# A hybrid attention and mLSTM layer on one core: remainders move from GpSimd to VectorE, row tiles by token halves, and the merge's seven products in another order

## The chip, the cores and the metric

One core of a Trainium2 chip runs the whole kernel. The metric is the device time of one execution in microseconds (us), as the median of several runs. Beside it stands the span of one profiled execution, from its first instruction to its last. The engines are named as in the profile: PE multiplies matrices, PEld loads its weights, DVE (VectorE) and ACT (ScalarE) work element by element, POOL is GpSimd, SP only issues DMAs.

## The reference

One layer on 1024 tokens of width 1024, all in float32:

```python
h = rms_norm(x) * (1 + sc_a) + sh_a                 # scales and shifts from the conditioning c
aq, ak, av, mq, mk, mv, mo, mi, mf, ga, gm = split(h @ w_in)
ya = diff_attention(...)                            # 8 heads, two softmaxes each, causal, with a bias
hm = mlstm_chunkwise(...)                           # 4 heads, matrix memory, after a short convolution of mq, mk
ym = sigmoid(mo) * rms_norm(hm)
merged = sigmoid(ga) * (ya @ w_a) + sigmoid(gm) * (ym @ w_m)
x = x + gt_a * (merged @ w_out)
h = rms_norm(x) * (1 + sc_f) + sh_f
x = x + gt_f * (square(relu(h @ w_ff1)) @ w_ff2)    # 1024 -> 4096 -> 1024
```

## The kernel before, in words

**Three products for one.** PE multiplies in a rounded format (fp32r). To keep float32's accuracy every operand is split in two: ACT writes the rounded high part, and a subtraction `src - high` makes the remainder (`split_lo`, L138). A product then costs three matmuls: high by high, high by remainder, remainder by high (`mm3` L165 to L167, `mm_block` L327). The subtraction runs on DVE or on POOL. `split_lo` takes an argument: true means POOL, false DVE, and none means every second one on POOL. Its callers `parts`, `add` and `sub` pass none through `pick`, which keeps two running loads and gives POOL a piece whenever DVE's load is well ahead.

**Weights of the projections.** `load_w` (L147 to L153) loads two stages `w_st` of 128x1024 by DMA, lets ACT write `w_hi` and subtracts into `w_lo`. `plan` is a list of such loads, and each product that takes its weights starts the next load. The entries of `plan` for the branch gates, for the queries and keys of each attention head (`qk_cols`), for the last values and for `w_m` say POOL.

**Seven products for eight.** The large products use Winograd's form of Strassen's scheme: a product of 2x2 blocks of 512 is made by seven block products, numbered 1 to 7, with sums of operand blocks before and sums of results behind them. The class `Group` does it for the projections and the first feed-forward product, the class `Chunks` for the merge product `ya @ w_a`, for `merged @ w_out` and for the second feed-forward product. A `Chunks` has a list of jobs, one per block product. `prep` makes the operand sums of a job and splits both operands into one of two sets of buffers (`s_op`, `t_op`); `run` lets PE do its 48 matmuls of 128x512 and calls `out` for each of four PSUM banks. The loop preps job n+1 before it runs job n, so a job's splits wait for the job two before it to release the buffers. Products 1, 5, 6 and 7 start new banks, 2, 3 and 4 accumulate on those of 1, 5 and 7.

**Orders.** The merge and the second feed-forward product run `ORDER_X` = (1, 7, 2, 4, 5, 6, 3), the product with `w_out` runs `ORDER_Y` = (1, 2, 5, 6, 3, 7, 4). `operands` has both sets of sums. In the merge, `out_a` adds the products into four quadrants of `merged` and calls `merge` for each piece: it fetches the gate and the other branch's part by DMA, takes a tanh on ACT, and does one multiply (L1288) and one add on DVE. For `w_out`, `out_o` adds into the rows `xr` of x, squares on ACT, and `rms` scales the rows for the next norm. `pieces` loads quadrants of weights, and multiplies those of `w_out` by the gate `gta` on DVE (L1672).

**Stages in time.** The norm of x and its transposed rows `hT`; projections as `Group`s until about 510 us; the four mLSTM heads until about 750 us; the eight attention heads until about 1290 us, each with the projection of the next head's queries and keys between its steps (`weave`); during the last head and after it the product of `ym` with `w_m`; the merge, the product with `w_out`, the first and the second feed-forward product.

**Row tiles.** `ActX` holds `hT` and later `ym` as four tiles of one pool with four buffers. A tile holds one part (high or remainder), four of the eight row blocks of 128 features, and all 1024 tokens. `reload` (L1273 to L1277) reads `ym` back from memory, a pair of row blocks and one token half at a time, as soon as `hT`'s buffers are free.

**Between the norm and the feed-forward products.** `norm_feat` transposes the scaled rows, `half0` splits them into the operands of products 1 and 2, and `right` makes the operand sums of the products 7, 5, 6, 3 and 4 (L312, then `parts`). These sums and splits go through `pick`. The order of this part is written out by hand as a string of letters.

The program is unrolled; a scheduler puts each engine's instructions in an order and adds the semaphores. An engine takes its own instructions in order.

Of the kernel before, what the change touches and what calls it, by code (L numbers as in the profile page):

```python
# [36 lines left out]
def kernel(  # L37
# [131 lines left out]
    class ActX:  # L169


        def __init__(self, name):
            self.t = [[xp.tile([P, 4, S], F32R, name=f"{name}{r}{i}", tag="x") for i in range(2)] for r in range(2)]

        def at(self, k, t0, n):
            return tuple(self.t[r][k // 4][:, k % 4, t0:t0 + n] for r in range(2))
# [350 lines left out]
    def modulate(q):  # L527
# [15 lines left out]
        def step(n):  # L543
# [9 lines left out]
            hh, hl = (hT.t[r][q][:, k:k + 2, m * 256:(m + 1) * 256] for r in range(2))  # L553
# [205 lines left out]
    class Conv(Group):  # L759
# [9 lines left out]
        def out(self, t, hf, n, a, b, into):  # L769
            c = crow[t][:, hf * 512:hf * 512 + 512]  # L770
            if b is None:
                nc.scalar.activation(c, a, AF.Copy)
            else:
                add(c, a, b, None if (t, hf) == (1, 1) else False)
            if (t, hf) in ((0, 1), (1, 0)):
                behind.extend(self.conv(t))
# [25 lines left out]
    class Gate(Group):  # L802
# [9 lines left out]
        def out(self, t, hf, n, a, b, into):  # L812
# [3 lines left out]
            if b is None:  # L816
                nc.scalar.activation(c, a, AF.Copy)
            else:
                add(c, a, b, None if (t, hf) == (1, 1) else False)
# [39 lines left out]
    def ml_in(h, hd):  # L859


        def half(hf):
# [7 lines left out]
            for i in (1, 0):  # L870
                for t in range(2):
                    d = hd["qk"][i, t, hf] = wt("r", [P, 2, 512], "qk", F32R)
                    parts((d[:, 0, :], d[:, 1, :]), hd["kc"][t][:, ts_] if i else q[:, t, :])

        def vals(g):
# [7 lines left out]
            parts((vt[:, :, 0, 0:256], vt[:, :, 1, 0:256]), vr)  # L883
# [212 lines left out]
    def at_v(h, vts):  # L1096
# [3 lines left out]
        def read(g):  # L1100
# [3 lines left out]
            parts((vt[:, :, 0, :], vt[:, :, 1, :]), vr.rearrange("p t (a d) -> p (t a) d", a=2))  # L1104
# [212 lines left out]
    def gate_cols(i):  # L1317
        cols((C_GA, C_GM)[i // 4] + (i % 4) * 256, True)

    def qk_cols(h):  # L1320
# [3 lines left out]
        plan.append(lambda: load_w([(srcs[q], lambda v, q=q: v[:, :, q * P:(q + 1) * P]) for q in range(2)], KT, True))  # L1324
# [6 lines left out]
    for h in range(AH):  # L1331
        if h % 2 == 0 and h // 2 not in (0, 1, 2):
            cols(C_AV + h * P, True)
# [4 lines left out]
    for u in range(4):  # L1338
        plan.append(lambda u=u: load_cols(w_m[0], u * 256, True))
# [142 lines left out]
    for h in range(AH):  # L1482
# [18 lines left out]
    class Chunks:  # L1501
# [6 lines left out]
        def __init__(self, xs):  # L1508
            self.n, self.jobs, self.made, self.tmp = 0, [], 0, {}
# [15 lines left out]
        def add(self, order, left, right, out, sums=None):  # L1525
            self.jobs += [(i, order, left, right, out, sums) for i in order]
# [9 lines left out]
        def prep(self):  # L1536
# [5 lines left out]
            i, order, left, right, _, sums = self.jobs[n]  # L1542
            s, t = self.s[n % 2], self.t[n % 2]
            for q in range(2):
                l, r = self.operands(i, order[1] == 7, left, right, sums, q)
                self.split(s(q), l)
                self.split(t(q), r)

        def operands(self, i, x, left, right, sums, q):
            b11, b12, b21, b22 = (right.get((m, q)) for m in (11, 12, 21, 22))  # L1550
            if sums is None:
                a11, a12, a21, a22 = (left[m, q] for m in (11, 12, 21, 22))
            two = range(2)

            def tmp(tag, name):
                return [wt(tag, [P, 512], name) for _ in two]
# [4 lines left out]
            r = {1: b11, 2: b21, 3: b22, 4: b21, 5: b12, 6: b11, 7: b12}[i]  # L1561
            if x:
                if i == 7:
                    r = tmp("f", "t3")
                    for k in two:
# [5 lines left out]
            elif i == 5:  # L1571
                r = self.tmp["r", q] = tmp("f", "t1")
                for k in two:
                    sub(r[k], b12[:, k], b11[:, k], False)
            elif i == 6:
                minus(b12, b22, b12)
                for k, v in enumerate(self.tmp["r", q]):
                    sub(b11[:, k], b22[:, k], v, False)
            elif i == 4:
                minus(b21, b21, b11)  # L1580
            if sums is not None:
                return sums(i, q), r
            l = {1: a11, 2: a12, 3: a12, 4: a22, 5: a21, 6: a11, 7: a21}[i]
            if i == 3:
                minus(a12, a12, a11)
            elif x:
                if i == 7:
                    l = tmp("m", "s3")
                    for k in two:
                        sub(l[k], a11[:, k], a21[:, k], False)  # L1590
                elif i == 5:
                    add(a21, a21, a22, False, 2)
                elif i == 6:
                    minus(a11, a21, a11)
            elif i == 5:
                l = self.tmp["l", q] = tmp("m", "s1")
                for k in two:
                    add(l[k], a21[:, k], a22[:, k], False)
            elif i == 6:
                minus(a21, a11, a21)  # L1600
                for k, v in enumerate(self.tmp["l", q]):
                    sub(a11[:, k], v, a11[:, k], False)
            return l, r

        def run(self):

            i, order, _, _, out, _ = self.jobs[self.n]
# [21 lines left out]
    ORDER_Y = (1, 2, 5, 6, 3, 7, 4)  # L1629
# [52 lines left out]
    def out_a(i, j, ps):  # L1682
        f0, f1 = j * P, 512 + j * P
        if i == 1:
            nc.scalar.activation(u1[:, j], ps, AF.Copy)
        elif i == 7:
            nc.scalar.activation(m22[:, j], ps, AF.Copy)
        elif i == 2:
            merge(m11[:, j], ps, f0, 0)
        elif i == 4:  # L1690
            add(m12[:, j], ps, u1[:, j], False)
        elif i == 5:
            add(m22[:, j], ps, m22[:, j], False)
            add(m22[:, j], m22[:, j], u1[:, j], False)
        elif i == 6:
# [384 lines left out]
```

## Time and profile before

| | |
|---|---|
| median of 3 runs | 2135.2 us (2126.42 to 2137.53) |
| the profiled execution | 2137.04 us, of which the span is 2135.2 us |
| mean granted TensorE clock | 0.970 |
| HBM read, written | 206.43 MB, 79.93 MB |
| queue q1 (hardware DMAs) | 41.8% of the DMA engines' time |

The page of the profile gives each engine's busy time, then the span in 40 slices, then the chain of work that ended last. Answers of the trace give the same by window of time, by group of equal instructions (how many, busy us, mean ns of one, idle time before them and what ended it) and one by one in order of time. A busy PE is not PE at its peak: back-to-back matmuls overlap in the records.

### The profile page before, as it was taken

What the parts mean: (1) busy time and instruction counts of PE and PEld (TensorE: products, weight loads), DVE (VectorE), ACT (ScalarE), POOL (GpSimd) and SP (SyncE); (2) the same over time, 40 slices, a digit from 0 to 9 for tenths busy, and PEclk for the clock granted to TensorE, in tenths of its full rate; (3) what the DMA queues carried; (4) which work ended last, traced back from release to release, by engine and by line L of the source; (5) the groups of instructions that cost most, each with busy time, mean ns of one, the idle gap of its engine ahead of it and who ended that gap; (6) DMA issues with size and microseconds to landing.
All of it is one profiled execution on the core that took longest, in us unless ns stands there. A gap on an engine that the chain in (4) does not pass through costs nothing. (4 is left out here: it accounts for less than half of the span.)

```text
span 2135.2 us, 30324 instructions
## 1 busy us (share of the span) xinstructions
PE 2001.3 (94%) x11201; PEld 1732.3 (81%) x11201; DVE 1660.5 (78%) x2887; ACT 1045.5 (49%) x1966; POOL 234.0 (11%) x251
## 2 busy tenths in 40 slices
PE   5889999999889999999999999888799999899999
PEld 5889898888778899898988788677678888788887
DVE  7876668987765468989877747998777667898896
ACT  5522234444565557777756634435444555433332
POOL 0000000002232211111112410004400000000000
PEclk7999999999999999999999999999899999999999
DMA  8354453235655342222222665503344445845432
GB/s 284 111 163 156 150 162 118 91 107 193 192 177 162 107 122 60 80 60 80 60 66 69 202 222 169 171 1 123 114 169 156 153 148 201 305 139 167 150 117 80
DMA packets 210634, 296.72 MB, mean 139 GB/s; under 512 B 14067, under 2 KB 132494, under 8 KB 210486
## 3 DMA queue, kind: packets, MB, share of 16 engines
q1 hardware_dynamic: 207542, 285.35, 41.8%
q0 software_dynamic: 2944, 9.44, 1.2%
q8 instruction: 88, 1.44, 0.3%
q14 instruction: 60, 0.49, 0.1%
HBM read 206.43 MB, written 79.93 MB: 134 GB/s over the span
## 5 line engine op out<-in xcount | busy, mean ns | idle before, releaser
L327 PE MATMUL cps<-t_op,s_op 128*128 128x512 f32 x2016 | 478.4, 398 | 27.3 <-ACT s_op L319 10.9
L327 PEld LDWEIGHTS cps<-t_op,s_op 128*128 128x128 f32 x2016 | 383.1, 191 | 119.6 <-ACT s_op L319 12.6
L319 ACT ACTIVATE w_op<-w_st 128x512 fp32r<-128x512 f32 (+1 forms) x192 | 130.6, 695 | 183.8 <-PE pb L327 57.8
L138 DVE TENSOR_TENSOR w_op<-w_st,w_op 128x512 fp32r<-128x512 f32 (+1 forms) x192 | 146.7, 784 | 6.3 <-ACT w_op L319 4.1
L165 PE MATMUL ps<-w_hi,hT 128*128 128x256 f32 x512 | 146.9, 287 | 0.0
L166 PE MATMUL ps<-w_lo,hT 128*128 128x256 f32 x512 | 146.7, 286 | 0.0
L167 PE MATMUL ps<-w_hi,hT 128*128 128x256 f32 x512 | 146.2, 286 | 0.0
L319 ACT ACTIVATE s_op<-act 128x1024 fp32r<-128x1024 f32 x56 | 58.4, 1051 | 142.9 <-PE cps L327 108.0
L138 POOL TENSOR_TENSOR w_lo<-w_st,w_hi 128x1024 fp32r<-128x1024 f32 x36 | 87.9, 2453 | 313.3 <-ACT w_hi L152 310.0
L1198 ACT ACTIVATE ee<-ee,mneg 128x256 f32<-128x256 f32 (+7 forms) x128 | 98.4, 770 | 21.0 <-DVE mneg L1194 20.6
L327 PE MATMUL pa<-b,w_op 128*128 128x512 f32 x384 | 96.4, 402 | 6.7 <-ACT m L430 6.6
L1188 PE MATMUL lg<-kb,qe 128*128 128x512 f32 (+3 forms) x384 | 96.1, 361 | 4.2 <-DVE kb L1160 1.9
L327 PE MATMUL pc<-bt,w_op 128*128 128x512 f32 x384 | 96.1, 396 | 3.8 <-DVE w_op L138 2.0
L166 PEld LDWEIGHTS ps<-w_lo,hT 128*128 128x128 f32 x512 | 98.0, 191 | 1.5 <-issue 0.9
L165 PEld LDWEIGHTS ps<-w_hi,hT 128*128 128x128 f32 x512 | 97.9, 191 | 0.8
L167 PEld LDWEIGHTS ps<-w_hi,hT 128*128 128x128 f32 x512 | 98.0, 191 | 0.2
L327 PEld LDWEIGHTS pa<-b,w_op 128*128 128x128 f32 x384 | 74.1, 194 | 23.1 <-ACT m L430 7.6
L327 PEld LDWEIGHTS pc<-bt,w_op 128*128 128x128 f32 x384 | 71.1, 188 | 24.6 <-DVE w_op L138 7.0
L315 DVE TENSOR_TENSOR acc<-cps,acc 128x512 f32<-128x512 f32 x116 | 76.9, 684 | 13.0 <-PE cps L327 12.8
L715 DVE SCALAR_TENSOR_TENSOR ac<-crow,cond,ac 128x256 f32<-128x256 f32 x112 | 54.0, 482 | 34.2 <-DMA crow<-in_w_ada_dram 32.5
L1194 DVE CUSTOM_DVE_ANT_0 ee<-lg,bs 128x512 f32<-128x512 f32 (+4 forms) x128 | 70.1, 559 | 12.4 <-PE lg L1188 11.4
L138 DVE TENSOR_TENSOR s_op<-act,s_op 128x1024 fp32r<-128x1024 f32 x56 | 68.2, 1219 | 5.4 <-ACT s_op L319 5.3
(418 smaller groups left out, 4948.8 us busy)
## 6 DMA issues: line engine op xcount, KB each, us to landing
w_st<-in_w_in_dram SPq DMA_DIRECT2D x72, 512.0 KB, 4.5
act<-act_d SPq DMA_DIRECT2D x56, 512.0 KB, 3.6
w_st<-in_w_ff_dram SPq DMA_DIRECT2D x36, 512.0 KB, 4.1
crow<-in_w_ada_dram SPq DMA_DIRECT2D x32, 512.0 KB, 3.9
w<-in_w_ff_dram SPq DMA_DIRECT2D x32, 512.0 KB, 5.0
act_d<-s SPq DMA_DIRECT2D x48, 256.0 KB, 2.0
wa<-in_w_ada_dram SPq DMA_DIRECT2D x16, 512.0 KB, 4.8
mq_d<-cv SPq DMA_DIRECT2D x16, 512.0 KB, 2.8
```

The source lines that it names most:

```text
L138: return (nc.gpsimd if pool else nc.vector).tensor_tensor(dst, src, hi.bitcast(F32), op=ALU.subtract)
L165: nc.tensor.matmul(o, lhsT=ah, rhs=bh, start=first, stop=False)
L166: nc.tensor.matmul(o, lhsT=ah, rhs=bl, start=False, stop=False)
L167: nc.tensor.matmul(o, lhsT=al, rhs=bh, start=False, stop=last)
L315: (nc.gpsimd if pick(pool, n) else nc.vector).tensor_tensor(o, a, b, op=ALU.add)
L319: nc.scalar.activation(dst[0], src, AF.Copy)
L327: nc.tensor.matmul(ps, lhsT=p, rhs=q, start=first and k == 0 and r == 0, stop=k == 3 and r == 2, skip_group_check=True,)
L715: nc.vector.scalar_tensor_tensor(ac, stv[:, k, :], cond[:, kk:kk + 1], ac, op0=ALU.mult, op1=ALU.add)
L1188: nc.tensor.matmul(lg[:, 0:max(256, w)], lhsT=hd["q"][hf][e][:, r, q4 * P:(q4 + 1) * P], rhs=hd["k"][e][:, c0:c0 + max(256, w)], start=r = ...
L1194: nc.vector.tensor_tensor_reduce(ee[:, c0:c0 + w], lg[:, 0:w], hd["bs"][:, n - c0 - w:n - c0][:, ::-1], -0.125, first, ALU.add, ALU.min, last,
L1198: nc.scalar.activation(ee[:, 0:n], ee[:, 0:n], AF.Exp, bias=mneg[:, e:e + 1], scale=-1.0, accum_out=ssum[:, e:e + 1])
```

## The change

- `split_lo`, `parts`, `add` and `sub` are told to use DVE wherever they were told to use POOL or were free to choose: the weights in `plan`, the reload of `ym`, the operands of the mLSTM heads, the values of attention, `half0` and `right`.
- `ActX` has one tile for each token half and part, with all eight row blocks.
- The merge runs (1, 2, 6, 7, 4, 5, 3), the product with `w_out` runs (1, 2, 6, 5, 3, 7, 4); the second feed-forward product stays as it was. All the sums of product 6 are made at its prep, in place but for one pair `t2`: those that its own operands need first, and three more (`behind`) after its splits. Product 7 then needs one more sum.
- In the merge the results are added 5 times for each column block instead of 7, and the four calls of `merge` come one at each of the products 2, 4, 5 and 3. For `w_out` it is 9 additions instead of 11, and one copy on ACT.
- The quadrants of `w_out` are loaded in the order 11, then 21, 12, 22.

```diff
 class ActX:
-            self.t = [[xp.tile([P, 4, S], F32R, name=f"{name}{r}{i}", tag="x") for i in range(2)] for r in range(2)]
+            self.t = [[xp.tile([P, KT, 512], F32R, name=f"{name}{r}{i}", tag="x") for r in range(2)] for i in range(2)]
...
-                    parts((d[:, 0, :], d[:, 1, :]), hd["kc"][t][:, ts_] if i else q[:, t, :])
+                    parts((d[:, 0, :], d[:, 1, :]), hd["kc"][t][:, ts_] if i else q[:, t, :], False)
...
-        cols((C_GA, C_GM)[i // 4] + (i % 4) * 256, True)
+        cols((C_GA, C_GM)[i // 4] + (i % 4) * 256, False)
...
-        plan.append(lambda u=u: load_cols(w_m[0], u * 256, True))
+        plan.append(lambda u=u: load_cols(w_m[0], u * 256, False))
...
-            filler += reload(ym, ym_d, True) + units[0:12 * 2]
+            filler += reload(ym, ym_d, False) + units[0:12 * 2]
...
+            a11, a12, a21, a22 = (left[m, q] for m in (11, 12, 21, 22))
+            l = {1: a11, 2: a12, 3: a12, 4: a22, 5: a21, 6: a11, 7: a11}[i]
+            r = {1: b11, 2: b21, 3: b22, 4: b21, 5: b12, 7: b11}.get(i)
+            if i == 6:
+                add(a21, a21, a22, False, 2)
+                minus(a11, a21, a11)
+                minus(b12, b12, b11)
+                r = [wt("f", [P, 512], "t2") for _ in range(2)]
+                for k in range(2):
+                    sub(r[k], b22[:, k], b12[:, k], False)
+                def rest():
+                    for k in range(2):
+                        sub(b21[:, k], b21[:, k], r[k], False)
+                        sub(b11[:, k], r[k], b11[:, k], False)
+                    minus(a12, a12, a11)
+                behind = (rest,)
+            elif i == 7:
+                minus(a11, a22, a11)
...
-    ORDER_Y = (1, 2, 5, 6, 3, 7, 4)
+    ORDER_Y = (1, 2, 6, 7, 4, 5, 3)
+    ORDER_Z = (1, 2, 6, 5, 3, 7, 4)
...
 def out_a(i, j, ps):
         elif i == 4:
             add(m12[:, j], ps, u1[:, j], False)
+            merge(m12[:, j], m12[:, j], f1, 0)
         elif i == 5:
             add(m22[:, j], ps, m22[:, j], False)
             add(m22[:, j], m22[:, j], u1[:, j], False)
-        elif i == 6:
-            add(m12[:, j], ps, m12[:, j], False)
-            add(m22[:, j], ps, m22[:, j], False)
-            add(u1[:, j], ps, u1[:, j], False)
-            merge(m12[:, j], m12[:, j], f1, 0)
             merge(m22[:, j], m22[:, j], f1, 512)
+        elif i == 6:
+            add(u1[:, j], ps, u1[:, j], False)
...
 def out_o(i, j, ps):
+                elif i == 6:
+                    add(u2[:, j], ps, u2[:, j], False)
                 elif i == 5:
-                    add(hi[:, c1], ps, hi[:, c1], False)
-                    for q in (lo[:, c1], hi[:, c0], hi[:, c1]):
-                        add(q, q, u2[:, j], False)
-                elif i == 6:
-                    for q in (lo[:, c1], hi[:, c0], hi[:, c1]):
-                        add(q, ps, q, False)
+                    nc.scalar.activation(u1[:, j], ps, AF.Copy)
                 elif i == 3:
+                    add(lo[:, c1], lo[:, c1], u2[:, j], False)
                     add(lo[:, c1], ps, lo[:, c1], False)
...
                 elif i == 7:
-                    add(hi[:, c1], ps, hi[:, c1], False)
+                    add(hi[:, c1], hi[:, c1], u2[:, j], False)
+                    add(u1[:, j], ps, u1[:, j], False)
+                    add(hi[:, c1], hi[:, c1], u1[:, j], False)
                     square(4 + j, 1)
                 else:
+                    add(hi[:, c0], hi[:, c0], u2[:, j], False)
                     add(hi[:, c0], ps, hi[:, c0], False)
...
 def half0(k):
-        parts(B[1 + k // 4](k % 4), e_at(k))
+        parts(B[1 + k // 4](k % 4), e_at(k), False)
...
-            sub(b21, b21, b22)
-        parts(B[i](k), src)
+            sub(b21, b21, b22, False)
+        parts(B[i](k), src, False)
```

More of the change, by code (lines that the diff above doesn't have):

```diff
@@ L552, in step @@
                     pin(nc.scalar.activation(vi, vi, AF.Identity, bias=b, scale=g))
-            hh, hl = (hT.t[r][q][:, k:k + 2, m * 256:(m + 1) * 256] for r in range(2))
+            ks = slice(q * 4 + k, q * 4 + k + 2)
+            hh, hl = (hT.t[m // 2][r][:, ks, m % 2 * 256:m % 2 * 256 + 256] for r in range(2))
             pin(nc.scalar.activation(hh, v, AF.Copy))
@@ L1323, in qk_cols @@
         ]
-        plan.append(lambda: load_w([(srcs[q], lambda v, q=q: v[:, :, q * P:(q + 1) * P]) for q in range(2)], KT, True))
+        plan.append(lambda: load_w([(srcs[q], lambda v, q=q: v[:, :, q * P:(q + 1) * P]) for q in range(2)], KT, False))
     AT_GATES = {}
@@ L1525, in add @@
         def add(self, order, left, right, out, sums=None):
-            self.jobs += [(i, order, left, right, out, sums) for i in order]
+            self.jobs += [(i, left, right, out, sums) for i in order]
         def split(self, dst, src):
@@ L1541, in prep, with operands @@
             self.made += 1
-            i, order, left, right, _, sums = self.jobs[n]
+            i, left, right, _, sums = self.jobs[n]
             s, t = self.s[n % 2], self.t[n % 2]
             for q in range(2):
-                l, r = self.operands(i, order[1] == 7, left, right, sums, q)
+                l, r, behind = self.operands(i, left, right, sums, q)
                 self.split(s(q), l)
                 self.split(t(q), r)
-        def operands(self, i, x, left, right, sums, q):
+                run(behind)
+        def operands(self, i, left, right, sums, q):
             b11, b12, b21, b22 = (right.get((m, q)) for m in (11, 12, 21, 22))
[L1551 to L1556, printed above, removed]
             def minus(o, a, b):
                 sub(o, a, b, False, 2)
-            r = {1: b11, 2: b21, 3: b22, 4: b21, 5: b12, 6: b11, 7: b12}[i]
-            if x:
+            if sums is not None:
+                r = {1: b11, 2: b21, 3: b22, 4: b21, 5: b12, 6: b11, 7: b12}[i]
                 if i == 7:
-                    r = tmp("f", "t3")
-                    for k in two:
+                    r = [wt("f", [P, 512], "t3") for _ in range(2)]
+                    for k in range(2):
                         sub(r[k], b22[:, k], b12[:, k], False)
@@ L1603, in operands @@
-            return l, r
+                return sums(i, q), r, ()
+            a11, a12, a21, a22 = (left[m, q] for m in (11, 12, 21, 22))
+            l = {1: a11, 2: a12, 3: a12, 4: a22, 5: a21, 6: a11, 7: a11}[i]
+            r = {1: b11, 2: b21, 3: b22, 4: b21, 5: b12, 7: b11}.get(i)
+            behind = ()
+            if i == 6:
[6 more added lines that the diff above has]
+                def rest():
+                    for k in range(2):
+                        sub(b21[:, k], b21[:, k], r[k], False)
[4 more added lines that the diff above has]
+                minus(a11, a22, a11)
@@ L1605, in run @@
+            return l, r, behind
         def run(self):
-            i, order, _, _, out, _ = self.jobs[self.n]
+            i, _, _, out, _ = self.jobs[self.n]
             s, t = self.s[self.n % 2], self.t[self.n % 2]
@@ L1711 @@
         if n == 4:
-            wo = pieces("e", "wo", w_out[0], False, (11, 12), behind)
+            wo = pieces("e", "wo", w_out[0], False, (11,), behind)
         ch.run()
         if n == 5:
-            pieces("v", "wo", w_out[0], False, (21, 22), behind, wo)
+            pieces("v", "wo", w_out[0], False, (21,), behind, wo)
+            pieces("e", "wo", w_out[0], False, (12,), behind, wo)
+            pieces("v", "wo", w_out[0], False, (22,), behind, wo)
             xr = fetch("r", "xr", x2, range(8))
```

60 lines of the change are left out of this document (14 added, 46 removed).

## The prediction

> **What bounds the kernel now.** I read the page first: the busy shares, then the slices of PE, DVE and POOL.
>
> ```profile
> PE 2001.3 (94%) x11201; PEld 1732.3 (81%) x11201; DVE 1660.5 (78%) x2887; ACT 1045.5 (49%) x1966; POOL 234.0 (11%) x251
> PE   5889999999889999999999999888799999899999
> DVE  7876668987765468989877747998777667898896
> POOL 0000000002232211111112410004400000000000
> ```
>
> PE bounds most of the span, and where its slice reads 9 nothing on DVE or POOL can move the time. It falls off at the start, in the mLSTM heads, in the last attention head, and in four slices from 1335 us on. DVE stands at 9 before those, POOL at 4 within. Next, the windows of these stages.
>
> ```profile
> 800.00:1100.00 300.00, 286.70 (x2191) 273.58 (x2190) 265.53 (x706) 220.03 (x549) 37.41 (x25) 0.99 0.25 70
> 1131.00:1151.00 20.00, 20.00 (x156) 19.36 (x156) 13.74 (x43) 12.10 (x29) 0.54 (x1) 1.00 0.04 14
> 1151.00:1210.00 59.00, 50.35 (x258) 39.55 (x257) 53.76 (x114) 44.06 (x106) 29.31 (x23) 0.94 0.54 170
> 1290.00:1367.00 77.00, 76.30 (x332) 61.83 (x331) 64.23 (x78) 34.67 (x45) 0.54 (x1) 1.00 0.58 187
> 1367.00:1460.00 93.00, 72.74 (x291) 56.59 (x289) 91.80 (x126) 38.92 (x59) 3.28 (x2) 0.91 0.16 57
> 1478.00:1550.00 72.00, 59.06 (x252) 46.98 (x250) 54.30 (x70) 36.39 (x65) 38.10 (x26) 0.91 0.38 125
> ```
>
> After the window and its length the columns are the busy times of PE, PEld, DVE, ACT, POOL, then the granted clock. From 1367 to 1460, at the end of the merge and in the product with `w_out`, DVE is busy 91.8 of 93 us and PE 72.7: DVE is the bound there. From 1478 to 1550, at the start of the feed-forward, PE loses 13 us while DVE and POOL share one chain. In the attention heads (800 to 1100) DVE is busy 89%.
>
> **What POOL costs DVE.** The order of time in the last head, then the groups of DVE:
>
> ```profile
> 1198.17 4.94 DVE L1204 SCALAR_TENSOR_TENSOR ssum<-ssum,nlam 128x1 f32<-128x1 f32 x1
> 1208.34 0.22 DVE L1204 SCALAR_TENSOR_TENSOR ssum<-ssum,nlam 128x1 f32<-128x1 f32 x1
> 1198.32 4.76 POOL L138 TENSOR_TENSOR w_lo<-w_st,w_hi 128x1024 fp32r<-128x1024 f32 x2
> L138 POOL TENSOR_TENSOR w_lo<-w_st,w_hi 128x1024 fp32r<-128x1024 f32 x36 | 87.9, 2453 | 313.3 <-ACT w_hi L152 310.0
> L271 DVE SCALAR_TENSOR_TENSOR nt<-nt 128x16 f32<-128x16 f32 x16 | 11.6, 723 | 0.3
> L271 DVE SCALAR_TENSOR_TENSOR nt<-nt 128x4 f32<-128x4 f32 x14 | 2.2, 160 | 0.1
> L270 DVE TENSOR_TENSOR nt<-rr 128x16 f32<-128x16 f32 x16 | 10.8, 674 | 0.7 <-ACT rr L269 0.6
> L270 DVE TENSOR_TENSOR nt<-ssy 128x4 f32<-128x4 f32 x14 | 2.8, 198 | 0.9 <-ACT ssy L269 0.7
> L315 DVE TENSOR_TENSOR acc<-cps,acc 128x512 f32<-128x512 f32 x116 | 76.9, 684 | 13.0 <-PE cps L327 12.8
> L138 DVE TENSOR_TENSOR s_op<-act,s_op 128x1024 fp32r<-128x1024 f32 x56 | 68.2, 1219 | 5.4 <-ACT s_op L319 5.3
> ```
>
> A DVE instruction on one column, 0.22 us otherwise, took 4.94 us, while two remainders ran on POOL. Such stalls count as busy DVE. The same shows in each head: `nt` of 16 columns takes 723 and 674 ns, of 4 columns 160 and 198. That is (563 + 476) ns x 16 = 16.6 us lost on two lines that meet the 16 `qk_cols` remainders, 1.04 us for each. So a weight remainder on POOL costs DVE at least 1.04 us there and at most its own 2.45; on DVE it costs 1.22. I take the low end, since most of DVE's other instructions in a head read PSUM and show no such stretch.
>
> The Trainium skill, "SBUF — State Buffer", section "Who interferes with whom", says that a DVE instruction with two SBUF inputs and a GpSimd instruction that reads SBUF exclude each other for the whole instruction, while a DVE instruction with at most one SBUF input goes on. The 4.94 us beside 4.76 agrees. By that rule taken alone each remainder costs DVE up to 2.45 us, which is the third rival below.
>
> **The change part by part.** All terms are against the profiled execution, 2137.0 us for a span of 2135.2; it lies 1.8 us over the median of the runs, 2135.2.
>
> *mLSTM heads.* Ten weight remainders (12.2 us on DVE) and twelve of 512 columns (12 x 0.69 = 8.2) come to DVE, and POOL's stretches go. DVE has the room (slices at 5 and 6), and PE waits here for other links. I take 0, with -4 to +4 as bounds.
>
> *Attention heads.* Two remainders a head, 2.44 us more for DVE, against 2.08 us of stretch that goes. The sums cancel, but not the place: `nt` stands on the chain to `raw`, for which PE waits.
>
> ```profile
> PE tp L1151 <- DVE raw L1142: 9.4, 4, 2.4
> 870.53 4.78 POOL L138 TENSOR_TENSOR w_lo<-w_st,w_hi 128x1024 fp32r<-128x1024 f32 x2 [6.07 <-ACT w_hi L152]
> 922.05 4.77 POOL L138 TENSOR_TENSOR w_lo<-w_st,w_hi 128x1024 fp32r<-128x1024 f32 x2 [6.53 <-ACT w_hi L152]
> ```
>
> Of those 9.4 us (waits from 800 to 1100) I take back 4. The added wait is that of a DVE remainder for ACT's `w_hi`: behind it on DVE stand the softmax's reductions. If all 2.44 us landed on the path, 8 heads would lose 20 us, less the 9.4: +10. Bounds -11 and +10, taken -4.
>
> *Row tiles and the last head.* The last read of `hT`'s first token half is two copies of `raw` before the end of its use, and yet all of `ym` waits for that end:
>
> ```profile
> 1131.03 0.58 ACT L1089 COPY raw<-ps 128x512 f32<-128x512 f32 x1 [3.85 <-PE ps L167]
> 1151.36 0.57 ACT L1089 COPY raw<-ps 128x512 f32<-128x512 f32 x1
> 1152.41 0.63 ACT L1276 ACTIVATE ym<-w_st 128x512 fp32r<-128x512 f32 x1
> L138 POOL TENSOR_TENSOR ym<-w_st,ym 128x512 fp32r<-128x512 f32 x16 | 21.3, 1350 | 22.8 <-ACT ym L1276 22.8
> ```
>
> With a tile for each token half, eight of the sixteen splits can run from 1131 on, where DVE is idle 6 of 20 us, instead of after 1151, where it is busy 91%. On DVE the sixteen cost 10.9 us; POOL's 21.3 us go, and at half of that as stretch the sum is nothing. PE loses 8.7 us from 1151 to 1210, and about 3.5 more to the clock (59 x 0.06). I take back 5; bounds 0 and -9.
>
> *Merge and `w_out`.* PE has 14 jobs of 48 matmuls. Its start, its stalls and the first matmul of the next stage, then two rows of DVE:
>
> ```profile
> 1289.02 2.96 PE L327 MATMUL cps<-t_op,s_op 128*128 128x512 f32 x12
> 1292.67 74.95 PE L327 MATMUL cps<-t_op,s_op 128*128 128x512 f32 x324 [0.70 <-DVE sg L1288]
> 1371.28 0.77 PE L327 MATMUL cps<-t_op,s_op 128*128 128x512 f32 x1 [3.66 <-DVE mg L315]
> 1378.14 45.83 PE L327 MATMUL cps<-t_op,s_op 128*128 128x512 f32 x191 [6.09 <-DVE t_op L138]
> 1429.92 15.70 PE L327 MATMUL cps<-t_op,s_op 128*128 128x512 f32 x55 [5.96 <-ACT s_op L319]
> 1460.42 6.75 PE L327 MATMUL cps<-t_op,s_op 128*128 128x512 f32 x16 [4.37 <-DVE xr L315]
> 1478.12 5.61 PE L327 MATMUL pa<-b,w_op 128*128 128x512 f32 x24
> 1369.26 1.88 DVE L315 TENSOR_TENSOR mg<-cps,mg 128x512 f32<-128x512 f32 x3
> 1373.46 2.35 DVE L1672 TENSOR_TENSOR wo<-wo,gta 128x1024 f32<-128x1024 f32 x2
> ```
>
> 324 matmuls in 74.95 us are 0.23 each, 11 us a job, so the stage could end near 1289 + 14 x 11 = 1443, plus 4 for transposes. It ends near 1478, where the next stage begins: 31 us lost to stalls and to the clock behind them (0.91). Back to back, three additions of 512 columns end after 1.88 us and two of 1024 after 2.35: beside the 0.684 and 1.219 of one, each further one takes 0.60 and 1.13. Operand sums stay at eight of 1024 columns per half in both products, so their total stays. Result additions fall by 2 x 4 x 0.60 = 4.8 us in each product, 9.6 together.
>
> Order does more. Before, product 6 of the merge puts 7 instructions on each of 4 blocks, 17 us of DVE in an 11 us job, and the next splits (`t_op`, 6.09 us) queue behind. After, no product has more than 4, 9.6 us a job. The sums for product 6, 16 us, come early, while DVE has 13 us free (64.2 of 77). So the first stall, 10 us, goes; so do those at 1429 and 1460, since the last four jobs carry 12 us of DVE at most each. What is late next is product 6 of `w_out`, third of its seven: behind the merge's last 7 us of results and a backlog of about 9 (product 5 of the merge 9.6, `gta` 6.8, splits 4.5, in an 11 us job), DVE must do one job's splits (4.5), the first sums of both halves (9.2), their splits (4.7) and three more sums (3.5). That is 31 to 38 us, where PE has two jobs, 22 us: a new stall of 8 to 16, and some 3 for the clock. 31 less 8 to 16 and 3 leaves 12 to 20; I take 15, bounds -4 (rival one) and -21.
>
> *Start of the feed-forward.* Thirty sums and splits leave POOL:
>
> ```profile
> 1500.95 0.69 PE L1785 MATMUL tp<-ksq,xr 128*128 128x128 f32 x2 [4.37 <-DVE rw L1790]
> 1515.58 5.49 PE L327 MATMUL pa<-b,w_op 128*128 128x512 f32 x12 [6.61 <-ACT m L430]
> 1510.40 3.99 POOL t L312
> L312 DVE TENSOR_TENSOR rw<-rw 128x512 f32<-128x512 f32 x3 | 4.2, 1388 | 7.5 <-POOL rw L312 3.8 <-POOL b L138 3.7
> ```
>
> The chain of work that ended last runs through POOL's `t`, and a sum of 512 columns takes DVE 1388 ns here, against 684. Moved, they cost 30 x 0.60 = 18 us of DVE; the stretch, by an estimate of 0.7 us (1388 less 684 ns) on 18 instructions, gives 13 back. From 1478 to 1550 DVE was busy 54.3; it would need about 54.3 - 13 + 18, less the eight splits that lie before 1478: 55. PE's 252 instructions there need at most 252 x 0.23 = 58. So the 72 us can shrink to about 60, DVE and PE both near full; I take 8 of the 12, since neither will be perfectly fed. Bounds 0 and -14.
>
> The conv and gate additions that could choose already ran on DVE (POOL has no row of L315), so that edit is nothing. Loads and the second feed-forward product keep their work.
>
> Sum: 0 - 4 - 5 - 15 - 8 = -32. 2135.2 - 32 = 2103 as a median.
>
> **The rivals.**
> One, the bound moves: DVE stays the bound from 1300 to 1550, and the new stall at product 6 of `w_out` eats most of what the first one gave, so the stage gains 4, the feed-forward 4, the heads and the last head 5: 2122. For it: DVE at 91.8 of 93.
> Two, slower: the remainders on DVE's queue delay the softmax by their whole length and the stretch that goes was never on the path. 8 heads x 2.44 = 20, half of the mLSTM's 20 another 10, less rival one's 8 and 5: +17, 2152. It decides if the heads' period, 51.5 us from 870.53 to 922.05, passes 53. Against it: PE's waits for `raw`. The Trainium skill, "Perfetto Trace Analysis", section "Optimizing Scalar/DVE Operations", says that with DVE saturated, moving work off it, even to GpSimd, may make sense, though between those two it might not help; this change goes the other way.
> Three, more: every POOL microsecond was lost to DVE. Then a head gets 4.78 back for 2.44, 2.3 us each, 19 in all instead of 4: 2088.
> Four, nothing to see: gains from 1300 to 1550 turn into waits for DVE further on, and the heads lose what the last head gains: 2130.
>
> **How the numbers follow.** Forecast 0.58 (2096 to 2112), rival one 0.18, two 0.08, three 0.09, four 0.07. A difference under 0.5%, 10.7 us, can hardly be told from none here. Rival one lies below that bound in most of its spread (0.15 of 0.18). Faster: 0.58 + 0.15 + 0.09 = 0.82; same 0.03 + 0.07 = 0.10; slower 0.08. The range leaves out rivals two and four and the far half of three: 2083 to 2128.
>
> **What would show it.** POOL busy under 70 us, `nt` of 16 columns near 200 ns. A head's period near 51. `ym` written from about 1132 on. PE without a stall at the change from the merge to `w_out`, one of 8 to 16 us two jobs on. 1478 to 1550 done in about 64 us. I am wrong if PE's waits for DVE in the heads grow, or if PE idles as long as before between the merge and the second feed-forward group.

## The result, and the profile after

The kernel after takes 2075.9 us (median of 4 runs, 2073.48 to 2083.83) against 2136.4 us (4 runs, 2126.42 to 2137.6): ratio 0.9733, 95% interval 0.9694 to 0.9773. That is 60 us less where 32 were forecast, below the range. The profiled execution took 2075.06 us, its span 2073.0. The page of the kernel after first, the busy times and three slices:

```profile
PE 1989.1 (96%) x11201; PEld 1723.2 (83%) x11201; DVE 1655.4 (80%) x2964; ACT 1045.0 (50%) x1966; POOL 59.3 (3%) x154
PE   5899999999999999999999899999899999999999
DVE  7976768889676568999978657999867667998896
POOL 0000000000011000000000110000000000000000
```

POOL loses 97 instructions and 175 us. DVE took them over, 36 of 1024 columns and 61 of 512, some 86 us at its own 1.22 and 0.69 us, and yet its busy time fell from 1660.5 to 1655.4 us. Some 10 us went with the shorter sums of the merge and `w_out` (the kernel with DVE alone, below, is busy 1665.8 us); by these figures the other 80, an estimate, were stretches of DVE's own instructions that ended. PE now reads 9 in all slices but the first two and two more.

To see where the 62 us of the span went I cut it at the same five points of the program in every kernel: the first `lps` matmul (542.7 us in both), the first `lg` matmul of head 0 and of head 7, the first of the merge and of the feed-forward, and the end of the latter's 336th. Windows of the kernel before, then of the kernel after: from and to, length, then busy PE, PEld, DVE, ACT, POOL, the granted clock.

```profile
542.70:787.40 244.70, 222.53 (x1389) 199.04 (x1387) 148.81 (x373) 136.65 (x325) 71.59 (x119) 0.95 0.51 151
787.40:1170.80 383.40, 363.83 (x2752) 344.94 (x2753) 325.76 (x859) 268.46 (x672) 53.91 (x37) 0.99 0.24 68
1170.80:1289.00 118.20, 112.75 (x548) 92.52 (x549) 74.81 (x145) 56.51 (x121) 37.02 (x34) 0.98 0.59 200
1289.00:1478.10 189.10, 167.72 (x705) 133.47 (x704) 169.80 (x221) 85.35 (x127) 11.99 (x10) 0.94 0.36 116
1478.10:1580.90 102.80, 86.77 (x370) 69.18 (x369) 75.84 (x103) 50.79 (x89) 38.00 (x26) 0.93 0.42 141
```

```profile
542.70:772.80 230.10, 216.39 (x1392) 193.17 (x1391) 151.06 (x394) 135.88 (x324) 26.23 (x94) 0.99 0.54 160
772.80:1136.00 363.20, 361.51 (x2756) 342.97 (x2757) 324.19 (x885) 269.11 (x676) 7.11 (x13) 1.00 0.27 74
1136.00:1253.10 117.10, 110.88 (x541) 92.24 (x541) 77.68 (x157) 53.90 (x115) 11.93 (x20) 0.96 0.62 204
1253.10:1420.20 167.10, 161.53 (x706) 129.61 (x705) 153.60 (x198) 84.17 (x126) 3.90 (x3) 0.99 0.36 119
1420.20:1519.20 99.00, 88.65 (x370) 70.18 (x369) 81.55 (x135) 53.81 (x93) 1.76 (x2) 0.93 0.47 156
```

| stage | forecast | before | after | difference |
|---|---|---|---|---|
| mLSTM heads | 0 | 244.7 | 230.1 | -14.6 |
| attention heads 0 to 6 | -4 | 383.4 | 363.2 | -20.2 |
| last head, `ym` by `w_m` | -5 | 118.2 | 117.1 | -1.1 |
| these two together | -9 | 501.6 | 480.3 | -21.3 |
| merge and `w_out` | -15 | 189.1 | 167.1 | -22.0 |
| start of the feed-forward | -8 | 102.8 | 99.0 | -3.8 |
| the rest | 0 | 1097.0 | 1096.5 | -0.5 |

The matmuls of `ym` by `w_m` fall partly before head 7's start and partly after it, so a kernel can shift work between those two stages (the counts behind PE's busy time tell how much); between kernels I compare their sum. In the attention heads PE was idle 19.6 us before (383.40 less 363.83) and is idle 1.7 us after. The groups of DVE and the one line of PE's waits from 800 to 1100 us, kernel after:

```profile
L272 DVE SCALAR_TENSOR_TENSOR nt<-nt 128x16 f32<-128x16 f32 x16 | 2.8, 173 | 0.3
L271 DVE TENSOR_TENSOR nt<-rr 128x16 f32<-128x16 f32 x16 | 2.7, 166 | 0.8 <-ACT rr L270 0.8
```

```profile
PE lg L1190 <- DVE mneg L1196: 0.8, 2, 0.5
```

`nt` of 16 columns went from 723 and 674 ns to 173 and 166, and the wait for `raw` is gone. `ym`, forecast to be written early, is: ACT's first split starts at 1098.8 us, in the kernel before at 1152.4.

```profile
L1278 ACT ACTIVATE ym<-w_st x16: 612/630/637, 1098.8 to 1145.8; 128x512 fp32r<-128x512 f32 x16
```

In the merge and the product with `w_out`, the rows of PE after a wait:

```profile
1332.84 27.72 PE L328 MATMUL cps<-t_op,s_op 128*128 128x512 f32 x118 [1.54 <-DVE t_op L138]
1363.29 1.40 PE L328 MATMUL cps<-t_op,s_op 128*128 128x512 f32 x4 [2.73 <-ACT t_op L320]
1364.99 6.92 PE L328 MATMUL cps<-t_op,s_op 128*128 128x512 f32 x24 [0.30 <-DVE t_op L138]
1372.59 38.52 PE L328 MATMUL cps<-t_op,s_op 128*128 128x512 f32 x166 [0.68 <-DVE t_op L138]
```

The stall of 3.66 and 6.09 us between the products is 1.54 us now. The new one at product 6 of `w_out` stands where the forecast had it, at 1363, but has 2.73 and 0.30 us instead of 8 to 16.

### The profile page after: what moved, and what is told of

The parts are those of the page before. It is cut to its first block, busy times and chain, and to the rows that moved or that the text cites. A ratio compares the mean times of both kernels' runs of the same rounds, so it can differ in the third digit from the quotient of the medians.

```text
span 2073.0 us, 30238 instructions
## 1 busy us (share of the span) xinstructions
PE 1989.1 (96%) x11201; PEld 1723.2 (83%) x11201; DVE 1655.4 (80%) x2964; ACT 1045.0 (50%) x1966; POOL 59.3 (3%) x154
## 4 chain that ended last, share of the span: by engine, by line
PE 62%; DVE 15%; DMA 11%; issue 6%; ACT 4%; POOL 1%; SPq 0%; DVEq 0%; POOLq 0%; ACTq 0%
PE cps L328 15%; PE pb L328 8%; PE pc L328 7%; PE pa L328 7%; PE pd L328 4%; DMA crow<-in_w_ada_dram 4%; PE ps L166 3%; PE ps L165 3%; PE ps L167 3%; PE lg L1190 3%; PE pv L1243 3%; DVE ac L717 2%; DMA ex<-ea_d 1%; PE tp L1223 1%; PE ops L579 1%
## 5 line engine op out<-in xcount | busy, mean ns | idle before, releaser
L328 PE MATMUL cps<-t_op,s_op 128*128 128x512 f32 x2016 | 471.9, 395 | 10.6 <-ACT s_op L320 5.2
L1190 PEld LDWEIGHTS lg<-kb,qe 128*128 128x128 f32 x384 | 61.5, 192 | 11.0 <-DVE mneg L1196 6.3
```

The costliest lines, as they stand in the source:

```text
L328: nc.tensor.matmul(ps, lhsT=p, rhs=q, start=first and k == 0 and r == 0, stop=k == 3 and r == 2, skip_group_check=True,)
L1190: nc.tensor.matmul(lg[:, 0:max(256, w)], lhsT=hd["q"][hf][e][:, r, q4 * P:(q4 + 1) * P], rhs=hd["k"][e][:, c0:c0 + max(256, w)], start=r = ...
```

## The experiments

The theory: a POOL instruction that reads two operands from SBUF shuts out DVE's two-operand instructions on SBUF, and the few that are shut out stand on PE's chain in both kinds of heads. The rivals: POOL's own result came late (latency); POOL's queue held up its small instructions; the gain came from the tiles or the orders; scatter.

**The parts alone.** The kernel before with one part of the change each: the engine (every `True` or free choice of the diff to `False`, nothing else), the merge with its orders and sums, the row tiles.

> The kernel before with only the engine changed: every remainder, sum and split that stood on POOL runs on DVE; row tiles, orders and operand sums as before. Theory (a POOL instruction that reads two SBUF operands shuts out DVE's two-operand instructions on SBUF, and the shut-out ones lie on PE's path in the mLSTM and attention heads): mLSTM heads -15, attention heads -20, start of the feed-forward -4, merge and w_out 0, in all about -39, some 2097 us. Rival A (the heads gained by something else in the change: row tiles or another order of work): -8 or less, the heads as before. Rival B (DVE's longer queue costs as much as the stretches): within 5 of before.

> The kernel before with only the new orders of the seven products, the operand sums in place and the fewer result additions in the merge and the product with w_out; POOL's remainders stay. Theory: the stage from the merge to the feed-forward gives about -20 by itself, and the heads do not move: about 2115 us. Rival A (the stage gains only since POOL is silent there): -5 or less.

> The kernel before with only the row tiles by token halves; ym's splits can start 20 us earlier, on POOL. Theory: the last head gains next to nothing, 0 to -3. Rival (my term in the forecast was right and the gain is elsewhere given back): -5 or more, seen as PE's busy share from 1151 to 1210 us going up.

Ratios to before: DVE alone 0.9855 (0.9835 to 0.9875), orders alone 0.9934 (0.9910 to 0.9957), tiles alone 0.9978 (0.9965 to 0.9992): some 31, 14 and 5 us, 50 of the 60; the other 10 belong to no part by itself. DVE and the orders gave less than I expected (39 and 20), the tiles more (0 to 3). In the mLSTM heads DVE alone takes 237.3 us, only 7.4 less than before where I expected 15; more on that stage below. Windows of DVE alone, from the attention heads on:

```profile
781.30:1142.30 361.00, 355.68 (x2722) 337.83 (x2722) 317.45 (x873) 264.31 (x667) 7.08 (x13) 1.00 0.25 68
1142.30:1267.50 125.20, 119.27 (x576) 98.94 (x575) 82.63 (x168) 58.97 (x125) 11.88 (x20) 0.96 0.60 201
1267.50:1456.20 188.70, 168.98 (x706) 134.07 (x706) 170.16 (x226) 85.27 (x127) 4.51 (x4) 0.93 0.35 117
1456.20:1548.40 92.20, 85.84 (x371) 69.07 (x370) 77.40 (x128) 51.78 (x91) 1.07 (x1) 0.94 0.47 157
```

The heads' gain is the engine's, and the merge stays as it was. The last head has 576 matmuls instead of 548 and the heads 30 fewer: `ym` comes later there. Heads and last head together take 486.2 us, 15.4 less than before; with the tiles, in the kernel after, 5.9 less again. The start of the feed-forward gains 10.6. Orders alone, the merge with `w_out` and the start of the feed-forward:

```profile
1282.80:1451.40 168.60, 162.19 (x706) 129.57 (x705) 157.32 (x200) 85.31 (x128) 9.75 (x8) 0.99 0.36 121
1451.40:1556.40 105.00, 88.52 (x370) 70.11 (x369) 87.97 (x113) 52.07 (x92) 33.46 (x22) 0.93 0.43 143
```

The merge and `w_out` give 20.5 us with POOL as noisy as before: that rival falls, and the term belongs to the orders, as the forecast had it. Some of it is handed on: DVE has 88.0 us in the start of the feed-forward instead of 75.8, and 2.2 us are lost there. Tiles alone, heads 0 to 6 and the last head:

```profile
783.40:1172.00 388.60, 367.56 (x2766) 348.05 (x2766) 328.54 (x861) 274.78 (x682) 65.30 (x46) 0.99 0.26 74
1172.00:1282.90 110.90, 107.13 (x537) 88.40 (x536) 64.44 (x145) 50.26 (x111) 25.16 (x26) 1.00 0.60 198
```

The last head is 7.3 us shorter, and the heads are 5.2 longer: 14 matmuls moved there, some 3 us, and `ym`'s splits on POOL now fall there too (65.30 us of POOL, not 53.91). The sum gives 2.1, the ratio 4.7. So the early release does something by itself; that POOL takes part of it back fits these figures but was not tried.

**The heads.** The query and key weights' remainders back on POOL; then two kernels that leave every remainder on DVE and let POOL do something useless beside each of the 16:

```diff
# pool_qk
-  plan.append(lambda: load_w([...], KT, False))
+  plan.append(lambda: load_w([...], KT, True))
# beside_read: after each of these remainders on DVE
+  for k in range(2):
+      nc.gpsimd.tensor_tensor(scr, sv[half k], hv[half k], op=ALU.subtract)   # 128x512, scr is read by nobody
# beside_write
+  nc.gpsimd.tensor_copy(scr[:, 0:1], hv[:, 0, 0:1])
+  for _ in range(6):
+      nc.gpsimd.memset(scr, 0.0)
```

> The kernel after with the 16 remainders of the attention heads' query and key weights back on POOL, nothing else. Theory: the heads lose most of their 20 us again, some +12 to +20 over after (2088 to 2096 us), the sums nt of 16 columns go back from near 200 to about 700 ns, and the mLSTM heads stay as in after. Rival B (the exchange of 1.04 us of stretch against 1.22 us of work is even, as forecast): +4 or less.

> The kernel after, with all its remainders on DVE, and beside each of the 16 remainders of the query and key weights POOL subtracts the same two operands into a scratch tile that nobody reads (two instructions of 128x512 each). Nothing waits for that result; DVE's work is what it was. Theory (a POOL instruction with two SBUF inputs shuts out DVE's two-operand instructions for its whole length, and that lies on PE's path): the heads lose, nt of 16 columns goes from near 200 to 500 ns or more, some +13 to +25 over after (2089 to 2101 us). Rival (what the heads lost before was the latency of POOL's own remainder, late for PE): 0 to +3.

> As the kernel with scratch subtractions, but POOL's instructions beside DVE's remainders only write (a copy of one column of the weights, so that they start at the same time, then six memsets of 128x512 bf16). Theory: nothing, within 5 us of after, nt of 16 columns stays near 200 ns. Rival (any POOL instruction, or its place in the program, slows DVE or PE): as with the scratch subtractions, +13 or more.

Medians 2098.2, 2090.9 and 2080.8 us; ratios 0.9828 (0.9808 to 0.9847), 0.9809 (0.9787 to 0.9831), 0.9751 (0.9731 to 0.9771); the kernel after was at 0.9733, and at 0.9726 (0.9701 to 0.9750) in a second measurement. Heads 0 to 6 of the three in this order:

```profile
784.20:1160.70 376.50, 365.21 (x2761) 347.39 (x2762) 326.23 (x876) 271.04 (x677) 30.99 (x23) 0.99 0.26 72
```

```profile
775.50:1150.80 375.30, 363.40 (x2757) 344.38 (x2758) 334.76 (x885) 269.62 (x676) 38.51 (x35) 1.00 0.26 73
```

```profile
774.90:1138.00 363.10, 361.49 (x2757) 342.94 (x2758) 324.31 (x885) 269.10 (x676) 47.61 (x93) 1.00 0.27 75
```

This is the verdict. Subtractions on POOL whose result nobody waits for cost the heads 12.1 us (375.3 against 363.2); the real remainders cost 13.3. If the heads had lost the latency of POOL's own remainders, scratch work would have cost nothing. The difference of 1.2 us doesn't measure latency, as POOL's time isn't the same in the two (38.51 and 30.99 us). But the real remainders show the stretch as well: in that window DVE has ten instructions of 1.21 us less to do than after, and is busy 2.0 us more, which is 14 us of stretch beside 13.3 us of time. That leaves little for latency. By the ratio they cost some 20 us, and `nt` went to 472 and 422 ns, less than the 700 that I had set.

More POOL time (47.61 us in that window) that only writes and reads single columns costs nothing. Twelve of the 32 scratch subtractions run before head 0; that stage took 234.7 us, which is within its scatter (see the mLSTM heads). DVE's groups and PE's wait beside the scratch subtractions:

```profile
L280 DVE TENSOR_TENSOR nt<-rr 128x16 f32<-128x16 f32 x16 | 5.3, 332 | 0.8 <-ACT rr L279 0.8
L281 DVE SCALAR_TENSOR_TENSOR nt<-nt 128x16 f32<-128x16 f32 x16 | 4.9, 307 | 0.3
```

```profile
PE tp L1162 <- DVE raw L1153: 7.4, 4, 2.1
```

The wait for `raw` is back. `nt` doubled, which is less than the 500 ns that I had set. In that stage DVE is busy 334.76 us instead of 324.19: 10.6 us of stretch, and 12.1 us of time. The two sums nearly agree, so most of what was stretched must have been on the path. (The subtractions also hold the load's stage buffer `w_st` until they are done, which the memsets don't. The next loads wait 8.8 us for them, but DVE waits 1.0 us for `w_hi` in both kernels, and none of PE's waits in these heads names a tile of weights.) The section of the Trainium skill that the prediction names ("SBUF — State Buffer", "Who interferes with whom") also says that a GpSimd instruction that only writes does not contend with a two-input DVE instruction; the 363.1 us agree.

**The last head.** The kernel after with `ym`'s and `w_m`'s remainders on POOL, and the kernel after with the old tiles.

> The kernel after with the sixteen remainders of ym and the eight of w_m (the last head and the product with them) back on POOL. The kernel with the row tiles alone took 7 us less than before from the last head to the merge, the one with DVE alone 7 us more: so after's -1 there may be a gain and a loss that cancel. Theory: that stage gains 3 to 7 against after (2069 to 2073 us). Rival (the stretch lies on the path there too, as in the other heads): +3 or more.

> The kernel after with the row tiles by rows and k halves as before. Theory (without the early release ym's sixteen splits crowd DVE after the last raw copy): +4 to +10, from the last attention head to the merge, as the kernel with DVE alone took 125.2 there against 117.1 of after. Rival (the tiles change nothing here): within 3 of after.

Ratios 0.9753 (0.9730 to 0.9775) and 0.9776 (0.9760 to 0.9792). Heads 0 to 6 and the last head, first with POOL, then with the old tiles:

```profile
773.80:1146.10 372.30, 363.53 (x2760) 342.57 (x2761) 326.97 (x874) 272.92 (x681) 34.49 (x32) 1.00 0.27 77
1146.10:1257.50 111.40, 106.79 (x538) 88.44 (x537) 68.86 (x144) 49.89 (x109) 24.78 (x26) 1.00 0.59 198
```

```profile
773.10:1134.40 361.30, 356.25 (x2721) 338.32 (x2722) 317.59 (x874) 264.69 (x667) 7.11 (x13) 0.99 0.25 68
1134.40:1260.10 125.70, 118.69 (x577) 98.40 (x576) 80.80 (x164) 58.76 (x124) 11.93 (x20) 0.97 0.64 208
```

On POOL the last head gains the 5.7 us that I expected, but heads 0 to 6 lose 9.1: together 483.7 us, 3.4 more than after, and by the ratio not to be told from it. My hope for a faster version fell. The old tiles take 487.0 us, 6.7 more than after: the tiles' 5 us of the forecast were there, together with DVE.

**The start of the feed-forward.** Its thirty sums and splits free to go to POOL again; and a version meant to be faster, four scalings of features from DVE to ACT (`norm_feat(range(4, 8), range(8), b_at)`).

> The kernel after with the thirty sums and splits at the start of the feed-forward free to go to POOL again. By the forecast's own term +8; by the profiled stages (before 102.8, after 99.0, with DVE alone 92.2 us) +4 to +10. Rival (DVE is the bound there and POOL's help is worth its stretch): 0 or faster.

> A version meant to beat after: at the start of the feed-forward, where DVE is the bound and ACT is half idle, the four transposed features of the second token half that DVE scales (0.72 us each) go to ACT. 4 x 0.72 = 2.9 us less on DVE's path: -1 to -3 (2073 to 2075 us) if DVE bounds it, 0 to +3 if ACT's splits of the weights wait behind them.

```profile
1420.20:1527.70 107.50, 91.86 (x371) 72.38 (x370) 88.17 (x113) 52.42 (x93) 33.49 (x22) 0.90 0.43 140
```

With POOL 0.9786 (0.9771 to 0.9800), some 11 us by the ratio, and the stage takes 107.5 us: moving this work is worth 8.5 by this pair, near the forecast. (In twelve kernels that do the same here the stage took 95.9 to 100.2 us.) The table shows 3.8 only because the new orders push work into this stage: with POOL's help from 102.8 to 105.0 (orders alone) and 107.5, without it from 92.2 (DVE alone) to 99.0. The version with ACT gave 0.9737 (0.9708 to 0.9766), not to be told from after.

**The mLSTM heads.** Their remainders (the gates' weights, queries, keys, values) back on POOL; then, as in the heads, scratch work beside DVE's remainders of gates and values, by a helper called after each:

```diff
# mlstm_read          nc.gpsimd.tensor_tensor(scr, src, hi, op=ALU.subtract)      # 36 of 128x512
# mlstm_write         nc.gpsimd.tensor_copy(scr[:, 0:1], one column of hi), then 3 x nc.gpsimd.memset(scr, 0.0)
# mlstm_write_x2      the copy, then 6 memsets;   mlstm_wait   the copy alone;   mlstm_busy   3 memsets alone
```

> The kernel after with the gate weights' remainders and the twelve of the mLSTM heads' queries, keys and values back on POOL. Theory (stretched DVE instructions lie on PE's path there, and a stalled PE also gets a lower clock): +8 to +14 over after, all of it ahead of the first attention head. Rival (the 14.6 us of the profiled runs are scatter of the granted clock in that stage and not POOL's): +4 or less.

> The kernel after; in the mLSTM heads POOL subtracts, beside each remainder of the gate weights and of the values, the same operands into a scratch tile that nobody reads (36 instructions of 128x512, some 57 us of POOL). DVE's own work stays. Theory (shut-out DVE instructions on PE's path, as in the attention heads): +8 to +17 over after, as with the remainders back on POOL there (2084 to 2093 us). Rival (the heads lost the latency of POOL's own remainders): 0 to +4.

> As the kernel with scratch subtractions in the mLSTM heads, with a one-column copy and three memsets of 128x512 bf16 in place of each. POOL's small instructions there (the masks of ex, the powers) queue behind them as long as behind the subtractions. Theory: 0 to +4. Rival C (in the mLSTM heads it was POOL's queue: the masks and powers waited for the remainders): as much as with the subtractions, +8 or more.

> The kernel after once more, unchanged, on the chip of the next three: what its time and its mLSTM stage scatter by. Theory: 2074 to 2080 us, and the mLSTM stage (230.1 us in its first profile, from the first matmul of the lps product to the first attention head) between 228 and 235.

> The kernel after with POOL's one-column copies alone in the mLSTM heads: POOL waits for ACT's high parts as its remainders did, and does next to nothing. Rival C in its narrow form (POOL's masks and powers stand behind an instruction that waits for ACT): as much as with copies and memsets, +5 to +10 over after. Theory: 0 to +3.

> The kernel after with the memsets alone in the mLSTM heads (108 of 0.53 us, waiting for nobody): POOL is occupied as by its remainders and reads nothing. Rival C in its wide form (POOL's own time delays its masks): +5 to +10 over after. Theory: 0 to +3; if both this and the copies alone give nothing, the +9 of the two together is scatter.

> The kernel with the copies and the memsets in the mLSTM heads, with six memsets in place of three: the suspected queue on POOL doubled, still nothing but a column read. Rival C (POOL's own time delays its masks and powers, on which PE's chain hangs): about twice the +9 of the single dose, +15 or more over after. Theory with scatter of the granted clock: 0 to +9, no more than the single dose.

| kernel | ratio to before (95%) | this stage, us | its granted clock |
|---|---|---|---|
| before | 1 | 244.7 | 0.95 |
| after | 0.9733 (0.9694 to 0.9773) | 230.1 | 0.99 |
| DVE alone | 0.9855 (0.9835 to 0.9875) | 237.3 | 0.96 |
| after once more | 0.9726 (0.9701 to 0.9750) | 231.3 | 0.99 |
| remainders on POOL | 0.9814 (0.9785 to 0.9843) | 239.4 | 0.97 |
| scratch subtractions | 0.9832 (0.9808 to 0.9857) | 249.8 | 0.95 |
| copies and memsets | 0.9775 (0.9755 to 0.9795) | 240.2 | 0.96 |
| copies, memsets doubled | 0.9789 (0.9762 to 0.9815) | 243.2 | 0.98 |
| copies alone | 0.9732 (0.9713 to 0.9751) | 232.4 | 0.97 |

The stage with scratch subtractions:

```profile
543.60:793.40 249.80, 226.67 (x1392) 200.82 (x1391) 170.79 (x397) 136.52 (x325) 69.77 (x124) 0.95 0.50 147
```

They cost 19.7 us in the stage, and DVE is busy 19.7 us more (170.79 against 151.06). By the ratio it is some 21, above the 8 to 17 expected. The narrow queue rival falls: waiting for ACT costs nothing. But time of POOL does cost something here, as it did not in the attention heads: the memsets cost some 9 us by ratio, doubled some 12, though DVE's busy time in the stage grows by only 2.4 and 4.4 us (153.49 and 155.46). My theory gave the single dose 0 to 4 and was too narrow; the doubled one fell between what I had set for theory (at most 9) and for the rival (15 or more). In the doubled kernel DVE waits for POOL's powers in the norm of the mLSTM's output:

```profile
DVE it L1032 <- POOL ssh L271: 13.9, 11, 2.9
```

In the kernel after that wait is 9.6 us in 11 times, 0.9 at most. The dose was doubled and the cost was not, and this stage scatters: in the version with ACT at the start of the feed-forward, which changes nothing here, it took 238.4 us at a clock of 0.97.

So the split of the 14.6 us stays partly open. In the profiled pair 8.5 us of it are PE's idle time (22.2 us before, 13.7 after), and 6.1 are longer busy time at a lower granted clock (0.95 against 0.99). The three kernels with all of before's POOL work here (before, orders alone, tiles alone) take 242.3 to 244.7 us, eight with none of it 230.1 to 238.4, DVE alone among them: on average the stage gains some 9 us, and the 14.6 of the one pair is partly scatter. The remainders back on POOL cost 17 us by the ratio, where 8 to 14 were expected, and 9.3 by the profiled stage. Shut-out DVE work is probably the larger part of it and POOL's queue the smaller, but no run here separates the two.

The memsets alone missed their aim. As they waited for nobody they ran in the first 72 us, delayed the stages ahead by 10 us (0.9775, 0.9756 to 0.9795), and say nothing about the queue in this one.

## Why the prediction was wrong, point by point

**mLSTM heads (0, measured -14.6).** "PE waits here for other links. I take 0." This step failed. The other links hang on DVE instructions too, and these were stretched: PE waits for `sw` in the product `num`, and `sw` took DVE 808 ns before and 688 after. PE's wait for it and the group of DVE, before, then after:

```profile
PE num L167 <- DVE sw L929: 8.5, 6, 2.4
L929 DVE TENSOR_TENSOR sw<-ex,sw 128x512 fp32r<-128x512 f32 x16 | 12.8, 808 | 6.3 <-ACT sw L928 6.2
PE num L167 <- DVE sw L931: 2.5, 5, 0.7
L931 DVE TENSOR_TENSOR sw<-ex,sw 128x512 fp32r<-128x512 f32 x16 | 11.0, 688 | 8.3 <-ACT sw L930 8.2
```

DVE at 5 and 6 tenths spoke for room, but room says nothing of a chain: PE was idle 22 of 244.7 us in that stage. How much of the 14.6 is this and how much scatter stays open; nearer 9 us is what all kernels together show.

**Attention heads (-4, measured -20.2, of which the engine alone 15.4 with the last head).** This step failed too, and one before it: "where its slice reads 9 nothing on DVE or POOL can move the time". All slices of these heads read 9, which is 90% or more, and 5% of their time went. "The sums cancel, but not the place" was the right thought, priced wrongly. I set 2.44 us of new DVE work against 2.08 of stretch and let 4 of 9.4 us of wait go. The stretch, 1.04 us a remainder by two lines of `nt`, was too small: back on POOL a remainder stretched DVE by 1.4 us (14 us for ten), as `raw` and `rr` behind `nt` were stretched too, 1325 and 277 ns instead of 1221 and 170. DVE's sum did cancel (325.76 and 324.19 us busy), but PE's waiting went whole, not by 4. The 9.4 was one row of PE's waits; the window quoted beside it had 13.3 us of PE idle in 300 (300.00 less 286.70), and over heads 0 to 6 there were 19.6. The heads' period of 51.5 us came from one pair of rows; it is 54.8 before (383.40 over seven heads) and 51.9 after. Rival three had the size, 19, by a wrong reason: not every POOL microsecond was lost to DVE (with scratch subtractions 31 us more of POOL, 38.51 less 7.11, stretched DVE by 10.6), but what was lost lay on the path.

**Row tiles and the last head (-5, measured -1.1; with the heads -9, measured -21.3).** Right: of the 21.3, the engine alone gives 15.4 and the tiles 5.9. The stage's own -1.1 has no meaning by itself, as part of `ym`'s product moves between the two.

**Merge and `w_out` (-15, measured -22.0).** Right in mechanism; the term that was too big is the new stall, 8 to 16 us against 3.0. Its length was taken from the wrong start, since PE didn't have to wait for both halves of product 6. DVE, kernel after:

```profile
1334.98 1.28 DVE L316 TENSOR_TENSOR mg<-cps,mg 128x512 f32<-128x512 f32 x2
1346.73 1.22 DVE L316 TENSOR_TENSOR mg<-mg,mg 128x1024 f32<-128x1024 f32 x1
1352.55 1.29 DVE L138 TENSOR_TENSOR t_op<-t,t_op 128x512 fp32r<-128x512 f32 x2
1364.25 1.29 DVE L138 TENSOR_TENSOR t_op<-t,t_op 128x512 fp32r<-128x512 f32 x2
```

PE ended the merge's matmuls at 1331.3. DVE still had 4 us of other work instead of the forecast's 9, began with the merge's last results at 1335.0 and with the first half's sums at 1346.7, and had the first half split at 1353.8, the second at 1365.5. The whole took it 30.5 us, near the 31 to 38 of the forecast. But PE began the product on the first half, and so was busy for 27.7 us in a row (the row at 1332.84) where the forecast gave it two jobs, 22 us. The wait for the second half is the stall.

**Start of the feed-forward (-8, measured -3.8).** The move was worth 8.5; what I left out is that the new orders of the stage before hand DVE work on, 2 to 7 us by the pairs above.

Against the forecast the mLSTM heads are 14.6 us off, the heads with the last head 12.3, the merge 7.0, the feed-forward 4.2 the other way, the rest 0.5: 30 in all. Of these, 27 lie in the stages where a stretch on PE's chain was priced too low; that price is shown for the attention heads, while in the mLSTM heads some of the difference is scatter.

## What to carry to other kernels

A stall is priced from the idle time of the engine that bounds the kernel, stage by stage, and not from the change in another engine's sum: 10.6 us of stretched DVE instructions, 3% of DVE's time in the heads, cost 12.1 us because they stood between PE and its next operand. To tell an engine's contention from its latency, let it do the same reads into a scratch tile beside the moved work, and then as much work that only writes. A stage whose work can move to the next is compared together with it.

## What was not expected of the hardware

In the attention heads the scratch subtractions stretched DVE by a third of the time that they took (10.6 of 31.4 us), in the mLSTM heads by nearly half (19.7 of 43.5, which is 69.77 less 26.23): most of DVE's instructions go on beside them. The real remainders of the query and key weights stretched it by more than half of theirs (14 of 23.9 us). Memsets that occupied POOL for longer stretched `nt` not at all:

```profile
L280 DVE SCALAR_TENSOR_TENSOR nt<-nt 128x16 f32<-128x16 f32 x16 | 2.8, 173 | 0.3
L279 DVE TENSOR_TENSOR nt<-rr 128x16 f32<-128x16 f32 x16 | 2.7, 166 | 0.8 <-ACT rr L278 0.8
```

A DVE instruction with a single SBUF input was held up too, in the kernel before: a `tensor_scalar` of 16 columns, 0.17 us otherwise, once took 2.19 beside two remainders on POOL (2.39 us each on average), and ended about when the first of them did. So the prediction's sentence that a DVE instruction with at most one SBUF input goes on did not hold without exception:

```profile
782.03 2.19 DVE L267 TENSOR_SCALAR nt<-rr 128x16 f32<-128x16 f32 x1
781.79 4.73 POOL L138 TENSOR_TENSOR w_lo<-w_st,w_hi 128x1024 fp32r<-128x1024 f32 x2 [5.86 <-ACT w_hi L152]
```

The mLSTM stage took between 230 and 238 us in kernels that do the same there, at granted clocks of 0.99 to 0.96.
